# Two groups of 384 columns instead of 448 and 320, and a higher priority for the split of a weight tile

## Chip, cores and metric

The kernel runs on one core of a Trainium2 chip. The metric is the device time of one launch in microseconds (us), the median of several runs. PE is TensorE, PEld its weight loads, DVE is VectorE, ACT is ScalarE, POOL is GpSimd, SP is SyncE, whose queue issues nearly all DMAs here.

## Reference

One inference step of a one-layer decoder with a model width of 1024: 2048 prompt tokens and 8 x 8 sample tokens, 2112 columns in all. What is computed, cut to its skeleton:

```python
proj = rms_norm(x) @ w_in                      # 1024 x 2464, 20 weight tiles
o_attn = sliding_window_attention(rope(q), rope(k), v, sinks)     # window 128
o_rw   = rwkv7(h_rw, ...)                      # recurrent, a 64 x 64 state per head
x = x + rms_norm(concat(o_attn, o_rw) @ w_out) # 8 weight tiles
gu = rms_norm(x) @ w_ffn_in                    # 44 weight tiles
hid = silu(conv3(gu[:, :2816])) * gu[:, 2816:]
x = x + rms_norm(hid @ w_ffn_out)              # 22 weight tiles
```

Everything is float32. The dense products are made of float32r halves: a tensor x is split into hi (rounded) and lo = x - hi, and each product is hi*hi + lo*hi + hi*lo, three matmuls.

## The kernel before

**Dense stages.** The 2112 columns are cut into five groups by `groups` (L61): 448, 448, 448, 448 and 320 columns; the last holds the 64 sample columns. Each group passes four kinds of stage: P (`project`, 20 tasks), O (`outproj`, 8 tasks), and the FFN as two stages, 60 and 6 tasks. A task is one weight tile of 128 x 1024 and 24 matmuls of 128 x 128 weights by the group's columns. All stages run in one written order:

```python
order = [P[0], P[1], P[2], O[0], P[3], F[0], O[1], F[1], P[4], F[2], O[2], F[3],
         O[3], F[4], F[5], O[4], F[6], F[7], F[8], F[9]]
```

F[2g] and F[2g+1] are the two FFN stages of group g.

**The weight tile's way.** `Dense.run` (L392) works on the tasks in order. In task i, after its second step, it emits `halves(i + 2)` (L411) and then `raw(i + 4)` (L406). `raw` is the DMA of a tile into one of two `w` buffers. `halves` takes one of three pairs of buffers `wh`, `wl` and calls `split` (L383): ACT casts w to wh, DVE subtracts to wl. So a split can start when its DMA has landed and when task i - 1, which read the buffers last, is done on PE; the next DMA needs the buffer that the split frees.

**Sides and mixer.** Between dense steps, a `Flow` (L234) emits two other streams of work. Sides are what follows an evicted product: token shift, rotary, `pair` (the factors of the recurrence), norms (`norm` L539, `rms` L805). The mixer does attention and the recurrence in eight units of 256 prompt columns and one for the samples, each in a window that is laid over the dense stages by their calculated cost (`Stage.cost`, L343). A stage can have to wait for others (`cond`, `cond2`): P needs the result of its `norm`, which reads x in `parts_of(n)` pieces (4 x 112 for 448 columns, 4 x 80 for 320, 3 x 128 for 384).

**Order on the engines.** The instructions of sides and mixer on PE stay in program order. On the other queues a scheduler chooses at compile time: each engine takes, of the instructions that are ready in its simulated run, the one with the lowest number of priority, which is the order of emission. `tc.high_priority(200)` sets the number of what is emitted under it 200 lower, so it goes ahead of up to 200 instructions emitted before it, on its engine, if it is ready. On the chip each queue then runs in the order written.

Of the kernel before, what the change touches and what calls it, by code (L numbers as in the profile page):

```python
# [32 lines left out]
CH = 64  # L33
# [3 lines left out]
GW, T, BW = 448, 256, 456  # L37
# [23 lines left out]
def groups(seq):  # L61

    n = seq + NS
    return [(t0, min(GW, n - t0), t0 + GW >= n) for t0 in range(0, n, GW)]


def parts_of(n):
# [13 lines left out]
class Shared:  # L81
# [26 lines left out]
    def derived(self):  # L108
# [17 lines left out]
        nc.gpsimd.memset(self.scanm.rearrange("p (c t) -> p c t", t=CH)[:, :, 0:1], 0.0)  # L126

        t0, n, _ = groups(self.seq)[-1]
        self.scans = cp.tile([128, n], F32, name="scans")
        nc.gpsimd.memset(self.scans, 1.0)  # L130
# [101 lines left out]
class Flow:  # L232
# [81 lines left out]
    def run(self, dense):  # L314
        for c in dense:
            if c is not None:
                self.force(c)
            self.tick()
        self.force(lambda: not (self.sides or self.mix or self.units or self.posts))
# [27 lines left out]
class Dense:  # L347
# [44 lines left out]
    def run(self, stages):  # L392

        nc = self.nc
        tasks = [t for s in stages for t in s.tasks]
        nt = len(tasks)
        raws, parts, starts, i = {}, {}, {}, 0
        for s in stages:
            starts[i] = s
            i += len(s.tasks)  # L400

        def view(i, t):
            m = tasks[i].m
            return t if m is None else t.rearrange("p (k m) -> p k m", m=128)[:, :, :m]

        def raw(i):  # L406
            if i < nt and i not in raws:
                raws[i] = view(i, self.W("w"))
                nc.sync.dma_start(out=raws[i], in_=tasks[i].src)

        def halves(i):  # L411
            if i < nt and i not in parts:
                raw(i)
                parts[i] = [view(i, self.sp.tile([128, D], F32R, tag=x, name=x, bufs=3)) for x in ("wh", "wl")]
                self.split(*parts[i], raws[i])

        first = stages[0]
        for k in range(KT):
            first.fetch(k)
            if k in (2, KT - 1):  # L420
                raw(k // 4)
        first.begin()
        halves(0)
        for k in range(KT):
            first.piece(k)
        yield None
        halves(1)
        for j in range(2, 4):
            raw(j)
        for i, t in enumerate(tasks):  # L430
            n1, n2, n6 = [starts.get(i + j) for j in (1, 2, 6)]
            if n6 and n6.begin:
                n6.begin()
            if n2:
                yield n2.cond
                yield n2.cond2
                if n2.piece:
                    yield from self.hold()
                    for k in range(3):
                        n2.fetch(k)  # L440
            wh, wl = parts[i]
            for k, c in enumerate(t.run(wh, wl)):
                if k == 1:
                    halves(i + 2)
                    raw(i + 4)
                if n1 and n1.piece:
                    n1.piece(k)
                    self.held = k < KT - 1
                yield c
# [44 lines left out]
    def project(self, g):  # L494

        sh, nc, a, v, te = self.sh, self.nc, self.a, self.nc.vector, self.te
        t0, n, sample = groups(sh.seq)[g]
        npr = n - NS if sample else n
        segs = [Seg(0, npr, 1, npr, CH, 0, sh.carry, sh.carry, sh.EC[:, t0 // CH:(t0 + npr) // CH])]
# [340 lines left out]
    def outproj(self, g, need):  # L840

        sh, nc, a, v = self.sh, self.nc, self.a, self.nc.vector
        t0, n, _ = groups(sh.seq)[g]
        m, st = [], {}
        S = Stage(n, cond=lambda: need <= self.done)
# [848 lines left out]
```

## Time and profile before

| | us |
|---|---|
| median of 3 runs | 2902.23 |
| lowest, highest | 2900.92, 2902.95 |
| profiled execution | 2901.7 |
| its span, first to last instruction | 2899.9 |

The profiled execution is 0.5 us under the median, and 1.8 us of it lie outside the span. Its mean granted TensorE clock is 0.965. All rows are of that one execution, and times in them count from the start of the span. A row of waits tells what an engine's idle time ended with.

### The profile page before, as it was taken

Reading aid. Unit: us, or ns where it says so; the run is one execution under the profiler, and the core shown is the slowest. Engines: PE = TensorE matmul, PEld = TensorE weight load, DVE = VectorE, ACT = ScalarE, POOL = GpSimd, SP = SyncE. Lnnn points to the kernel's source line nnn. Section 1 sums busy time; section 2 is a strip of 40 time slices with the busy share of each in tenths; the row PEclk is TensorE's granted clock in tenths of the full one; section 3 lists DMA queues with packets and bytes.
Section 4 is the critical chain, followed back from the end, with each engine's and each line's share of the span. In section 5 each row is a group of like instructions: output and inputs, shape, how many; then the busy total and the mean of one; then the engine's idle time right before and its main releaser. Section 6 shows DMA issues by size and latency. Waiting matters only on the chain.

```text
span 2899.9 us, 46282 instructions
## 1 busy us (share of the span) xinstructions
PE 2749.9 (95%) x16993; PEld 2344.2 (81%) x16993; DVE 1934.6 (67%) x3792; ACT 1410.0 (49%) x2630; POOL 239.9 (8%) x519
## 2 busy tenths in 40 slices
PE   8898995999999999978999999999999999999997
PEld 6676783667888888857887888888899999999997
DVE  6677685586874674696874575788645774557666
ACT  6455553455564455445754446554333453334543
POOL 1011010001000000003100000000001000101111
PEclk9998996799999999989999999999999999999998
DMA  6566664347744434456744335475333563335443
GB/s 211 156 202 168 189 180 128 121 137 219 209 138 140 125 108 148 142 155 188 230 129 136 117 120 169 156 233 164 122 112 107 178 192 109 104 108 182 158 148 120
DMA packets 310530, 446.58 MB, mean 154 GB/s; under 512 B 118536, under 2 KB 238952, under 8 KB 310288
## 3 DMA queue, kind: packets, MB, share of 16 engines
q1 hardware_dynamic: 309872, 443.48, 49.5%
q8 instruction: 134, 2.20, 0.3%
q14 instruction: 92, 0.75, 0.1%
q10 hardware_dynamic: 432, 0.16, 0.0%
HBM read 362.19 MB, written 76.97 MB: 151 GB/s over the span
## 4 chain that ended last, share of the span: by engine, by line
PE 81%; DVE 9%; DMA 4%; issue 3%; ACT 2%; SPq 1%; DVEq 0%; ACTq 0%
PE gm L213 50%; PE pf L213 17%; PE pc L184 3%; PE po L184 1%; DVE wl L386 1%; PE sc L184 1%; PE pz L184 1%; PE ppt L184 1%; SPq L1089 1%; DVE tmp L1075 1%; DVE tt L1076 1%; PE pu L184 1%; PE pS L184 1%; DMA r<-x2d 1%; PE sc_e L184 1%
## 5 line engine op out<-in xcount | busy, mean ns | idle before, releaser
L213 PE MATMUL gm<-xhi,wh 128*128 128x448 f32 (+3 forms) x2880 | 1062.1, 371 | 32.0 <-ACT wh L385 17.2
L213 PE MATMUL gm<-xhi,wl 128*128 128x448 f32 (+3 forms) x2880 | 1035.2, 360 | 11.5 <-DVE wl L386 11.5
L213 PE MATMUL gm<-xlo,wh 128*128 128x448 f32 (+3 forms) x2880 | 1039.5, 361 | 6.5 <-DVE xlo L386 6.1
L385 ACT CAST wh<-w 128x1024 fp32r<-128x1024 f32 (+1 forms) x470 | 489.4, 1042 | 708.0 <-PE gm L213 321.2
L386 DVE TENSOR_TENSOR wl<-w,wh 128x1024 fp32r<-128x1024 f32 (+1 forms) x470 | 569.9, 1213 | 375.3 <-ACT wh L385 362.6
L213 PEld LDWEIGHTS gm<-xhi,wh 128*128 128x128 f32 (+2 forms) x2880 | 543.4, 189 | 117.4 <-issue 30.1
L213 PEld LDWEIGHTS gm<-xlo,wh 128*128 128x128 f32 (+2 forms) x2880 | 544.6, 189 | 60.2 <-DVE xlo L386 12.7
L213 PEld LDWEIGHTS gm<-xhi,wl 128*128 128x128 f32 (+2 forms) x2880 | 544.3, 189 | 57.7 <-DVE wl L386 15.0
L213 PE MATMUL pf<-hh,wh 128*128 128x448 f32 (+1 forms) x880 | 319.5, 363 | 2.1 <-DVE acc L942 1.7
L213 PE MATMUL pf<-hl,wh 128*128 128x448 f32 (+1 forms) x880 | 313.1, 356 | 0.0
L213 PE MATMUL pf<-hh,wl 128*128 128x448 f32 (+1 forms) x880 | 312.6, 355 | 0.0
L915 POOL COPY zcar<-zz 128x2 f32<-128x2 f32 x110 | 79.1, 719 | 1467.4 <-ACT zz L904 1467.4
L942 DVE TENSOR_TENSOR acc<-acc,pf 128x448 f32<-128x448 f32 (+1 forms) x200 | 117.7, 591 | 112.1 <-PE pf L213 111.2
L213 PEld LDWEIGHTS pf<-hh,wh 128*128 128x128 f32 x880 | 165.3, 188 | 25.4 <-issue 6.7
L213 PEld LDWEIGHTS pf<-hh,wl 128*128 128x128 f32 x880 | 165.2, 188 | 12.1 <-issue 0.7
L213 PEld LDWEIGHTS pf<-hl,wh 128*128 128x128 f32 x880 | 165.5, 188 | 11.5 <-issue 1.7
L911 DVE SCALAR_TENSOR_TENSOR c<-zz,c_cw,c 128x448 f32<-128x448 f32 (+1 forms) x220 | 140.8, 640 | 22.4 <-ACT c L905 18.8
L925 DVE TENSOR_TENSOR c<-c,gm 128x448 f32<-128x448 f32 (+1 forms) x110 | 65.1, 592 | 121.0 <-PE gm L213 103.2
L918 ACT ACTIVATE c<-c 128x448 f32<-128x448 f32 (+1 forms) x110 | 61.3, 557 | 126.7 <-DVE c L911 93.4
L1075 DVE TENSOR_TENSOR tmp<-gb,tt 64x31 f32<-64x31 f32 (+21 forms) x279 | 92.2, 331 | 12.4 <-DMA gb<-dgr 8.8
L386 DVE TENSOR_TENSOR xlo<-r,xhi 128x448 fp32r<-128x448 f32 (+1 forms) x112 | 64.2, 591 | 47.8 <-ACT xhi L385 47.6
L1076 DVE TENSOR_TENSOR tt<-tt,tmp 64x31 f32<-64x31 f32 (+21 forms) x279 | 92.4, 331 | 3.5
(272 smaller groups left out, 3082.3 us busy)
## 6 DMA issues: line engine op xcount, KB each, us to landing
w<-in_w SPq DMA_DIRECT2D x220, 512.0 KB
w<-in_w2q SPq DMA_DIRECT2D x100, 512.0 KB
w<-in_w_all SPq DMA_DIRECT2D x90, 512.0 KB
ab<-abd SPq DMA_DIRECT2D x66, 512.0 KB
w<-in_w_out SPq DMA_DIRECT2D x40, 512.0 KB
r<-in_xT SPq DMA_DIRECT2D x56, 224.0 KB
r<-od SPq DMA_DIRECT2D x32, 224.0 KB
x2d<-mx SPq DMA_DIRECT2D x32, 224.0 KB
```

What stands on the lines that cost most here:

```text
L184: return self.tc.keep_in_program_order(f(*args, **kw))
L213: return self.te.matmul(out, lhsT, rhs, **kw)
L385: self.nc.scalar.copy(out=hi, in_=src)
L386: self.nc.vector.tensor_tensor(out=lo, in0=src, in1=hi.bitcast(F32), op=ALU.subtract)
L911: v.scalar_tensor_tensor(out=c[:, :npr], in0=z[:, j:j + npr], scalar=cw(j), in1=c[:, :npr], op0=ALU.mult, op1=ALU.add)
L915: nc.gpsimd.tensor_copy(out=sh.zcar[:, f, :], in_=z[:, npr:npr + 2])
L918: nc.scalar.activation(out=c, in_=c, func=AF.Silu)
L925: v.tensor_tensor(out=c, in0=c, in1=ps, op=ALU.mult)
L942: v.tensor_tensor(out=accs[c], in0=accs[c], in1=ps, op=ALU.add)
L1075: v.tensor_tensor(out=tm, in0=col, in1=row, op=ALU.mult)
L1076: v.tensor_tensor(out=tt[:nb, w:, 0:w], in0=tt[:nb, w:, 0:w], in1=tm, op=ALU.subtract)
L1089: nc.sync.dma_start(out=x, in_=y)
```

## The change

The last two groups get the same width: 768 remaining columns are cut at a multiple of 64, into 384 and 384 (the last keeps the 64 sample columns, and has 320 prompt columns instead of 256). And the two instructions of a weight tile's split are emitted under a higher priority; the tile's DMA is not.

```diff
 def groups(seq):
 
     n = seq + NS
-    return [(t0, min(GW, n - t0), t0 + GW >= n) for t0 in range(0, n, GW)]
+    starts = list(range(0, n, GW))
+    left = n - starts[-2]
+    starts[-1] = starts[-2] + (left + CH) // (2 * CH) * CH
+    return [(t0, t1 - t0, t1 == n) for t0, t1 in zip(starts, starts[1:] + [n])]
...
                 parts[i] = [view(i, self.sp.tile([128, D], F32R, tag=x, name=x, bufs=3)) for x in ("wh", "wl")]
-                self.split(*parts[i], raws[i])
+                with self.tc.high_priority(200):
+                    self.split(*parts[i], raws[i])
```

## Rows read from the trace of the kernel before

**Rows 1.** The page, whole span: busy time of two engines; chain that ended last, by engine.

```profile
PE 2749.9 (95%) x16993; PEld 2344.2 (81%) x16993; DVE 1934.6 (67%) x3792; ACT 1410.0 (49%) x2630; POOL 239.9 (8%) x519
...
PE 81%; DVE 9%; DMA 4%; issue 3%; ACT 2%; SPq 1%; DVEq 0%; ACTq 0%
```

**Rows 2.** Windows by stage: P0; F1; P4; F9. Stretch, length, busy (count), clock, DMA.

```profile
0.00:140.00 140.00, 116.46 (x508) 95.30 (x509) 91.24 (x160) 74.02 (x131) 12.14 (x49) 0.95 0.61 184
...
1203.00:1274.00 71.00, 55.97 (x290) 41.04 (x289) 63.89 (x161) 32.58 (x83) 1.41 (x4) 0.92 0.63 190
1274.00:1399.00 125.00, 110.68 (x884) 94.86 (x885) 91.45 (x216) 69.73 (x161) 31.60 (x63) 0.89 0.58 173
...
2859.00:2900.00 41.00, 23.41 (x156) 22.16 (x154) 25.82 (x59) 9.12 (x15) 0.00 (x0) 0.81 0.30 95
```

**Rows 3.** Windows of steady FFN at 448 and 320 columns: PE, PEld, DVE, ACT, POOL.

```profile
2450.00:2500.00 50.00, 50.00 (x245) 45.56 (x244) 24.89 (x31) 19.42 (x27) 5.35 (x8) 1.00 0.33 106
...
2700.00:2750.00 50.00, 50.00 (x343) 50.00 (x343) 31.54 (x53) 22.75 (x39) 8.14 (x20) 1.00 0.47 151
```

**Rows 4.** Waits of PE, 20 to 140 us (P0): total us, times, longest.

```profile
PE gm L213 <- DVE wl L386: 9.3, 4, 5.6
PE rb_ps L184 <- DVE bk L771: 4.3, 1, 4.3
```

**Rows 5.** Waits of PE, 1274 to 1400 us (P4).

```profile
PE gm L213 <- ACT wh L385: 9.7, 2, 7.7
...
PE gm L213 <- DVE wl L386: 1.3, 2, 1.0
```

**Rows 6.** Timeline of DVE, 86 to 103 us (P0): start, length, instruction.

```profile
95.17 0.62 DVE L513 TENSOR_TENSOR hs<-gm,rb 128x448 f32<-128x448 f32 x1 [4.33 <-PE gm L213]
...
99.50 0.62 DVE L651 TENSOR_TENSOR qk<-qk,qsw 128x448 f32<-128x448 f32 x1
100.04 2.35 DVE L386 TENSOR_TENSOR wl<-w,wh 128x1024 fp32r<-128x1024 f32 x2
```

**Rows 7.** Timeline of PE, 94 to 109 us.

```profile
101.32 0.74 PE L213 MATMUL gm<-xhi,wl 128*128 128x448 f32 x1 [5.56 <-DVE wl L386]
101.86 0.57 PE L213 MATMUL gm<-xhi,wh 128*128 128x448 f32 x1
...
105.59 0.57 PE L213 MATMUL gm<-xlo,wh 128*128 128x448 f32 x1
```

**Rows 8.** Timeline of SP's queue, 1318 to 1342 us (P4).

```profile
1326.23 3.94 SPq L1089 DMA_DIRECT2D G<-dxr  x8
...
1331.68 0.38 SPq L409 DMA_DIRECT2D w<-in_w_all  x1
```

**Rows 9.** Timeline of ACT, the same stretch.

```profile
1337.37 1.04 ACT L385 CAST wh<-w 128x1024 fp32r<-128x1024 f32 x1 [6.02 <-DMA w<-in_w_all]
```

**Rows 10.** Waits of PE, 1203 to 1274 us (F1, ahead of P4).

```profile
PE ms L184 <- DVE sa L803: 5.3, 1, 5.3
PE rb_ps L184 <- DVE dg L568: 5.3, 1, 5.3
```

**Rows 11.** Timeline of DVE, 1264 to 1275 us (the norm ahead of P4).

```profile
1266.79 1.22 DVE L386 TENSOR_TENSOR wl<-w,wh 128x1024 fp32r<-128x1024 f32 x1
...
1269.68 0.48 DVE L568 TENSOR_TENSOR dg<-c_ident,rs 80x320 f32<-80x320 f32 x1
```

**Rows 12.** Waits of ACT, whole span.

```profile
ACT wh L385 <- PE gm L213: 321.2, 166, 8.7
```

**Rows 13.** Groups by line and form, whole span: busy us, mean ns, idle before.

```profile
L386 DVE TENSOR_TENSOR wl<-w,wh 128x1024 fp32r<-128x1024 f32 x460 | 561.7, 1222 | 375.3 <-ACT wh L385 362.6 <-DMA dgr<-G 4.1 <-PE pu L184 4.0
...
L973 DVE SCALAR_TENSOR_TENSOR acc<-acc,c_gT,rb 128x448 f32<-128x448 f32 x32 | 20.9, 676 | 1.4 <-ACT rb L823 1.4
```

**Rows 14.** Groups by line and form, 2875 to 2900 us (the end).

```profile
L973 DVE SCALAR_TENSOR_TENSOR acc<-acc,c_gT,rb 128x320 f32<-128x320 f32 x8 | 4.1, 547 | 2.0 <-ACT rb L823 2.0
```

## The prediction

> **What bounds the kernel now.** I read the page first, for the engine that sets the time: PE is busy for 2749.9 of 2899.9 us and has 81% of the chain that ended last [rows 1]. So the time is PE's work, plus some 150 us in which it stands still, plus what a lowered clock adds to the work after a stop. The reader should see that DVE at 67% over the whole says little, because the next view, the windows by stage, shows where the standing still lies: the FFN stages run PE without a gap [rows 3], while P0 is idle for 140 - 116.5 = 23.5 us, F1 for 15.0, P4 for 14.3 and the last stage for 17.6 [rows 2]. In F1 DVE is busy for 63.9 of 71 us, so there DVE is the bound; in P0 no engine is full, so there it is order and latency. Third, the waits of PE in those windows give the reason of each stop, and fourth, timelines of the queue that was late show what stood ahead of the late instruction. These two views carry the sum.
>
> **The widths: PE.** No instruction count of the dense products changes; each group has 94 tasks of 24 matmuls, 2256, before and after. What could change is the time of one. In two steady FFN windows one matmul goes every 50/245 = 0.204 us at 448 columns and every 50/343 = 0.146 us at 320 [rows 3]. The quotient is 0.714, that of the widths as well (320/448). So the time is proportional to the columns with no fixed part that these rows show, 384 columns should take 0.175 us, and 2 x 0.175 equals 0.204 + 0.146. This term is zero; the counts are whole instructions, so it is known to about 0.5%, and the 0.35 us a pair over 2256 pairs makes that some 4 us either way.
>
> The weight loads do not set a floor in these rows: a load is recorded with 45.56/244 = 0.187 us at 448 columns, and yet matmuls, each with a load of its own, follow each other at 0.146 us at 320 [rows 3]. The Trainium skill, "TensorE: Matmul & The Clock Gate", section "Back-to-back issue gap", says that in a stream of load and matmul pairs the spacing is set by both, which would make a narrow matmul wait for its load. If the recorded 0.187 us were such a floor, two groups of 384 would save 0.204 + 0.187 - 2 x 0.187 = 0.017 us on 2256 pairs, 38 us; the spacing of 0.146 us rules it out nearly entirely.
>
> **The widths: everything else.** DVE and ACT work of the two groups is nearly proportional to columns too, but moves from P3, O3 and the FFN of group 3 to those of group 4. Three effects have a size.
>
> (a) P4 gains slack. A split may run from the end of task i - 1 to the start of task i + 2, two tasks: 48 x 0.146 = 7.0 us now, 8.4 us at 384 columns. It needs 1.04 (the cast [rows 9]) and 1.22 us (the subtraction [rows 13]). This helps the same waits as the priority; I count it there.
>
> (b) The norm ahead of P3 and P4 reads 3 pieces instead of 4. Ahead of P4 PE stands still for 5.3 us until `dg`, the last step of that norm [rows 10]. One piece less is worth at least nothing and at most that whole wait; the yields in `norm` give a piece 3 of about 17 us, so I take 2 us off. Ahead of P3 the norm has a whole O stage as cover: nothing; without that cover it would be the same 2 us.
>
> (c) The end gets longer. After the last matmul come about ten DVE steps on the group's width, then the norm and its output. One step takes 676 ns at 448 and 547 ns at 320 columns [rows 13, 14], 1.0 ns a column, so 384 costs 0.065 us more each: 16 steps of the final norm and some more ahead of it, 1.0 to 1.5 us, plus wider matmuls of the norm at half clock (0.81 granted on average there, 1.2 GHz for a part of it [rows 2]). I take 1.5 us, bounds 1 and 3.
>
> **The priority.** It adds and removes no instruction. It can only take away PE's waits for `wh` and `wl`, and it can only lengthen others, as DVE and ACT do the same work in another order.
>
> In P0 PE waits for `wl` four times, 9.3 us [rows 4]. The longest shows how: `wl` could not start before 100.04 us, because it stood in DVE's queue behind `hs`, which itself waited until 95.17 for PE, and then behind seven further instructions of sides, from `qk` to `qk` [rows 6]. PE stopped for 5.56 us and came back at half clock: ten matmuls in 105.59 - 101.86 = 3.73 us, 0.373 each where 0.204 is the rule, 1.2 instead of 2.4 GHz [rows 7]. That adds (0.373 - 0.204) x 11 = 1.9 us to this stop. P0's weight waits with their clock are about 9.3 + 3 = 12 us. In P4 it is 9.7 + 1.3 = 11.0 us [rows 5]; at a mean clock of 0.89 over 125 us [rows 2] 13.8 us of full clock are missing, nearly half of that while PE stands still anyhow, so about 5 us go with the weight waits. P4 together: 16 us. The most that the priority and the slack can take away is 28 us; the least is nothing, if the scheduler put the splits late because in its run their data was late.
>
> What of it is queue order? In P0 the subtraction was passed over by work emitted earlier, which 200 numbers of priority reach; but the cast ahead of it was late too, and a transfer that is late in the scheduler's run is not helped. I take half, 6 us. In P4 7.7 of the 11.0 us are one stop, and that one is a DMA's: ACT waited 6.0 us for w [rows 9], whose DMA was issued at 1331.68 behind eight issues of the recurrence that held SP for 3.9 us and others ahead [rows 8]. The DMA's priority is not raised; an earlier split frees its buffer earlier and may let it be issued ahead of that block. With its clock this stop is some 11 us; I take a third, 4 us. The rest of P4, 3.3 us and 1.5 of clock, is queue order at ACT and DVE: 5 us, all of it.
>
> Against that, what does a split that goes first delay? Behind it stand the sides and the mixer's evictions. In the FFN stages PE has no waits that it could lengthen, the lags of the mixer cover 1.2 us. But ahead of P1, P2 and P4, PE waits for a chain on DVE: 4.3 us ahead of P1 [rows 4], and ahead of P4 5.3 us for `sa` and 5.3 us for `dg` [rows 10]. Already now one `wl` of 1.22 us lies in the chain that ends with that `dg` [rows 11]. I count one more split for each of these three places, 3.7 us with the clock about 4. Bounds: nothing, and 15 us (three splits at each place are 11 us, and 4 us of half clock).
>
> **Sum.** -6 - 4 - 5 (weight waits) - 2 (norm) + 1.5 (end) + 4 (delays) = -11.5 us. Against the profiled execution's own 2901.7 us this gives 2890.2; the median stands 0.5 us above that execution, so 2891 us, -0.4%.
>
> **Rivals.**
>
> *The waits move.* The splits come earlier and PE stops at the next thing that is late: in P0 the norm ahead of P1, in P4 the recurrence's transfers. For it speaks that no engine's work shrinks and that P4's largest stop is a DMA's [rows 9]; against it that P0's `wl` had its operands long before [rows 6]. Time: 2902 within 6 us.
>
> *Slower: split first, chain late.* Place: F1 and the start of P4, where DVE has no room (63.9 of 71 us). Each split put ahead delays a chain that PE already waits for by 1.22 us. ACT stands idle for 321 us in front of casts whose buffer PE has not yet freed, 166 times [rows 12]; a cast that is put still earlier in ACT's queue holds up what follows it. The skill's same page, section "Architectural detail", states that ACT's and DVE's queues are strictly first in, first out; the trace agrees, since `wl` stood behind a waiting `hs` [rows 6]. It decides as soon as the chains of the three places lose more than the 15.5 us that the other terms give: four more splits at each, 14.6 us, with the clock. If PE merely waits for the chain where it waited for weights, three at each are enough: 2902 + 11 + 4 - 2 + 1.5, about 2916 us.
>
> *Much faster.* All weight waits go, the block at SP included, and P4's norm is no longer waited for: -28 - 5 + 1.5, 2870 us.
>
> *The narrow matmuls had a floor:* 2902 - 38, 2864 us; the spacing speaks against it.
>
> **How the numbers follow.** About 0.2% (6 us) is what a measurement of this kernel can tell from no change. My forecast, faster by 6 to 20 us: 0.42. Much faster: 0.12, and the floor 0.02. The waits move, within 6 us: 0.21. Slower: 0.23, because after P3 the emission of all sides and units shifts as well. So faster 0.56, same 0.21, slower 0.23. The likeliest case alone reaches from 2882 to 2896. The range takes in the rival below nearly whole and the one above up to its worked-out time: 2869 to 2916.
>
> **What would show it.** In the changed profile: matmuls of group 3 and 4 every 0.175 us, with the dense time of both together unchanged; PE's waits for `wh` and `wl` in P0 and P4 below 12 us instead of 20; the stop at 101 us gone or short; the wait for `dg` ahead of P4 within 3 us of today's 5.3; the stretch after the last matmul 1 to 2 us longer. Wrong would be the forecast if the waits for `dg`, `bk` and `sa` grew by more than those for weights shrank, if SP still held P4's weights back for 8 us, or if the mixer's units fell elsewhere after P3 and opened a stop that today's trace does not have.

## The result, and the profile after

The changed kernel takes 2924.96 us, median of 4 runs (2920.32 to 2932.91), where the kernel before takes 2902.59 beside it (2900.92 to 2904.54, 4 runs): a ratio of 1.0072, interval 1.0054 to 1.0090. That is slower by 21 us, above the whole range that was forecast. Below, a ratio is always against the kernel before on the same chip, and 0.1% is 2.9 us. One profiled execution stands within some 8 us of its kernel's median, so totals are read from ratios and places from profiles. That of the changed kernel took 2932.9 us; its span is 2931.1.

The page of the kernel after, its busy time and its chain, beside [rows 1]:

```profile
PE 2767.6 (94%) x16979; PEld 2392.5 (82%) x16979; DVE 1939.8 (66%) x3792; ACT 1412.0 (48%) x2618; POOL 241.4 (8%) x519
...
PE 43%; DVE 3%; DMA 2%; issue 1%; ACT 0%; SPq 0%; DVEq 0%; ACTq 0%
```

PE's busy time grew by 17.7 us for the same products, and the span without busy time from 150.0 to 163.5 us. So the loss of this execution has two halves: more standing still, and matmuls that take longer, at a lower granted clock (0.957 over the execution, 0.965 before). A part of the second half belongs to this execution alone, which is 8 us above its median: in O0 it has 40.7 us at the lower clock where the kernel before had 28.2, with 5.3 and 5.0 us of standing still. The chain could be followed back only through half of the span this time and is not used.

Windows of the kernel after, in order P0, P1, F1, P4, steady FFN at 384 columns, and the last stage (columns as in [rows 2]):

```profile
0.00:123.00 123.00, 112.08 (x507) 92.52 (x508) 91.11 (x159) 74.34 (x131) 14.58 (x49) 1.00 0.70 205
123.00:287.00 164.00, 141.05 (x779) 109.33 (x779) 120.77 (x254) 82.68 (x182) 18.76 (x38) 0.91 0.62 177
1204.00:1276.00 72.00, 59.28 (x286) 44.36 (x285) 59.32 (x137) 29.66 (x70) 1.82 (x4) 0.85 0.64 192
1276.00:1426.00 150.00, 135.06 (x984) 111.98 (x984) 111.96 (x261) 81.75 (x184) 19.42 (x68) 0.91 0.55 167
2632.00:2884.00 252.00, 251.87 (x1450) 251.31 (x1449) 149.06 (x249) 108.40 (x181) 40.45 (x86) 1.00 0.44 139
2884.00:2931.00 47.00, 27.87 (x154) 26.35 (x152) 28.98 (x58) 9.46 (x15) 0.00 (x0) 0.82 0.28 90
```

P0 ends at 123 instead of 140 us, with full clock. P1 takes 164 us where it took 156. P4 holds 984 matmuls in 150 us; before it held 884 in 125 [rows 2]. The steady FFN gives 252/1450 = 0.174 us a matmul, as forecast.

PE's waits after, first in P0 (20 to 123 us), then in P1, then in P4 (1276 to 1426 us):

```profile
PE gm L216 <- DVE wl L389: 0.5, 1, 0.5
```

```profile
PE pz L187 <- DMA zt<-dtr: 9.9, 5, 7.2
PE pd L187 <- ACT tha L755: 5.6, 1, 5.6
PE rb_ps L187 <- DVE bk L775: 3.8, 1, 3.8
```

```profile
PE ppt L187 <- DVE nr L53: 7.7, 1, 7.7
PE ss_ps L187 <- ACT k L618: 4.3, 1, 4.3
PE gm L216 <- ACT xhi L388: 2.8, 1, 2.8
```

The waits for weights are gone: 9.3 us in P0 have become 0.5 [rows 4], 11.0 in P4 none [rows 5]. The priority did what it says. In P4 two new ones of 7.7 and 4.3 us stand in their place (`xhi` had 3.2 us before), and in P1 there is a new one of 5.6 us for `tha`. PE stands still in P4 for 14.9 us, before for 13.9.

### The profile page after: what moved, and what is told of

The parts are those of the page before. It is cut to its first block, busy times and chain, and to the rows that moved or that the text cites. A ratio compares the mean times of both kernels' runs of the same rounds, so it can differ in the third digit from the quotient of the medians.

```text
span 2931.1 us, 46214 instructions
## 1 busy us (share of the span) xinstructions
PE 2767.6 (94%) x16979; PEld 2392.5 (82%) x16979; DVE 1939.8 (66%) x3792; ACT 1412.0 (48%) x2618; POOL 241.4 (8%) x519
## 5 line engine op out<-in xcount | busy, mean ns | idle before, releaser
L216 PE MATMUL gm<-xlo,wh 128*128 128x448 f32 (+4 forms) x2880 | 1040.1, 362 | 2.8 <-DVE xlo L389 2.7
L216 PE MATMUL gm<-xhi,wl 128*128 128x448 f32 (+4 forms) x2880 | 1037.0, 360 | 0.8 <-DVE wl L389 0.8
L919 POOL COPY zcar<-zz 128x2 f32<-128x2 f32 x110 | 87.0, 791 | 1464.0 <-ACT zz L908 1464.0
L915 DVE SCALAR_TENSOR_TENSOR c<-zz,c_cw,c 128x448 f32<-128x448 f32 (+2 forms) x220 | 140.8, 640 | 15.9 <-ACT c L909 13.3
```

Of the source, the lines that this page charges most:

```text
L216: return self.te.matmul(out, lhsT, rhs, **kw)
L915: v.scalar_tensor_tensor(out=c[:, :npr], in0=z[:, j:j + npr], scalar=cw(j), in1=c[:, :npr], op0=ALU.mult, op1=ALU.add)
L919: nc.gpsimd.tensor_copy(out=sh.zcar[:, f, :], in_=z[:, npr:npr + 2])
```

## Experiments

"Old widths" are those of the kernel before.

**The two parts alone.** The first kernel has only the diff in `groups`, the second only the priority.

> The widths alone: groups of 384 and 384, no priority. If the loss of 22 us comes from the widths (the mixer's and the sides' work falls elsewhere after P3), this takes 2915 to 2930 us, with the waits for wh and wl in P0 as before (9.3 us) and new stops only after 606 us. If the loss comes from the priority, it takes 2895 to 2906 us. If the two only lose together, both parts alone are near 2903.

> The priority alone: groups of 448 and 320. If the loss comes from the priority, this takes 2912 to 2930 us, with P0 about 17 us shorter and P1, P2 and O0 together as much longer, so that O0 ends at 606 to 609 us, and with further loss in P4 or after. If the loss comes from the widths, it takes 2885 to 2905 us: P0's gain is given back by the end of O0, P4's weight waits go.

Widths alone: ratio 1.0051 (1.0033 to 1.0069). Priority alone: 1.0037 (1.0023 to 1.0052). Both lose, and their sum, 0.88%, is within the interval of the whole change. So as far as these intervals tell, the two losses add up, and each can be studied alone.

**Is any other order of work a loss?** The spacing between steps of the sides is a little longer:

```diff
-    LAG, GAP = 2500.0, 1400.0
+    LAG, GAP = 2500.0, 1500.0
```

> Old widths, no priority; the shortest spacing that the emission keeps between steps of the sides is 1500 instead of 1400 of its units. No work changes, on PE steps of sides move by some matmuls, the counts by stage stay, DVE has about a quarter of its instructions elsewhere. Theory C (the kernel before is one of few good arrangements, and any other costs some us in new small stops): 2907 to 2916 us, with stops in other places. Rival D (a change of order alone is worth little, and widths and priority lost for reasons of their own): 2899 to 2906 us.

Ratio 0.9989 (0.9973 to 1.0004). Rival D holds for this one other order: it costs nothing. That any other order would cost something is not borne out, and the reasons are looked for in the two parts themselves.

**The priority, by place.** First the 20 tiles of P0 alone, then those of P0 and P4, then all but P1's:

```diff
-                with self.tc.high_priority(200):
+                with self.tc.high_priority(200 if i < len(first.tasks) else 0):
```

> Old widths; the split has its higher priority only for the 20 weight tiles of P0, all later tiles keep the old order. With the priority everywhere P0 ended 17 us earlier, and at the end of O0 9 us of it were left. Theory A (later splits pass later chains): without them P1, P2 and O0 lose little, so O0 ends 9 to 17 us before that of the kernel before and the rest is as before: 2885 to 2893 us. Rival B (what is won in P0 is waited away in P1 to O0, because the chain of the first units sets their end): O0 ends less than 5 us earlier, 2898 to 2904 us.

> Old widths, the split's priority for the tiles of P0 and of P4, the two stages whose weight waits the prediction counted. If P4's 11 us of weight waits are worth anything by themselves: 5 to 10 us below the kernel with P0's tiles alone, 2883 to 2889 us against a kernel before of 2902. If other chains stand right behind them, as P4 with all tiles raised took the same 125 us: within 4 us of that kernel, 2889 to 2897 us.

> Old widths, the split's priority everywhere but for P1's 20 tiles (transfers as they are). The kernel with P0's tiles alone gained 10 us, the one with all tiles lost 7. If nearly all of these 17 us is P1's, as the profiles have it (10 us by stage, the rest within what clock and chance move): 2892 to 2900 us, P1 at 153 to 157 us. If later stages lose as much by their own splits: 2901 to 2908 us.

The ratios are 0.9965 (0.9952 to 0.9978), 0.9961 (0.9946 to 0.9975) and 1.0000 (0.9985 to 1.0016). So P0's part gains 10 us; it is P1 and the other stages that lose. Durations of the stages in the profiles, us, each from its first dense matmul to the next stage's (P0 from the start):

```
                     P0     P1     P2    P3     F0    P4   |  ratio
before             139.9  156.1  215.4  160.1  387.8 125.0 |  1
P0 alone           123.4  153.3  223.1  165.4  388.9 125.5 |  0.9965
P0 and P4          123.1  154.1  225.3  165.6  389.8 123.7 |  0.9961
all but P1         121.9  153.8  221.3  164.7  392.0 124.3 |  1.0000
all                123.0  163.3  219.8  164.6  390.9 125.1 |  1.0037
```

P0 gains 17 us, and 8 of them are given back in P2 (it takes 219 us or more in every profile whose P0 takes 125 us or less, and 213 to 216 in the others whose second group is as before). P3's 5 us are not the priority's: the kernel with the longer spacing has them too (165.6 us). With all tiles raised P1 loses 10 us. "All but P1" does not have that loss, and yet the kernel as a whole has not P0's gain either, which the first guess (nearly all in P1) did not expect: some 10 us go to the splits from P2 on, in small amounts. By the profiles, PE stands still for 150.6 us in all where it is 142.5 with P0 alone, most of it in P3 (14.8 instead of 10.4 us) and F0 (3.4 instead of 1.5).

Two kinds of wait grew most: for `h`, an eviction on ACT, and for `dg`, the last step of a norm on DVE. PE's waits over the whole span, with P0 alone and with all but P1:

```profile
PE gm L213 <- ACT h L709: 2.9, 3, 1.4
PE ms L184 <- DVE dg L818: 3.0, 1, 3.0
```

```profile
PE gm L213 <- ACT h L709: 11.7, 5, 5.9
PE ms L184 <- DVE dg L818: 10.0, 4, 3.2
```

Against these 15.8 us, waits for `wh` went from 18.0 to 10.4 us and others shrank too.

P4's waits, with P0's tiles raised, and with P0's and P4's:

```profile
PE gm L213 <- ACT wh L385: 10.3, 2, 8.4
```

```profile
PE gm L213 <- ACT h L709: 5.0, 2, 4.0
PE gm L213 <- ACT xhi L385: 3.0, 2, 2.7
...
PE gm L213 <- ACT wh L385: 1.7, 1, 1.7
```

Of 11.6 us of waits for weights (10.3 for `wh`, 1.3 for `wl`) 9.9 go, PE stands still in P4 for 10.5 instead of 14.0 us, P4 takes 1.8 us less, and the kernel is not measurably faster. Of the longest new stop, for `h` until 1294.28 us, ACT's timeline (P0 and P4 raised) shows what stands ahead: two casts, which ended at 1291.38, and a softmax behind them.

```profile
1289.39 1.99 ACT L385 CAST wh<-w 128x1024 fp32r<-128x1024 f32 x2 [1.29 <-PE gm L213]
...
1293.77 0.46 ACT L709 COPY h<-gm 64x256 f32<-64x256 f32 x2
```

Right behind P4's weight waits stood other waits, which took up about two thirds of what was won.

**The priority, by engine.** The cast and the subtraction raised one at a time (the call of `split` written out, one of its two lines under the priority).

> Old widths; only the subtraction on DVE has the higher priority, the cast on ACT keeps the old order. P0's waits were for wl, which is DVE's. Theory A1 (the loss comes from casts that stand first in ACT's queue and wait for a buffer): P0 keeps most of its 17 us and the stops for ACT's evictions do not come, 2888 to 2897 us. Rival A2 (the loss comes from DVE's chains that a split passes): as with the whole priority, 2907 to 2916 us.

> Old widths; only the cast on ACT has the higher priority, the subtraction on DVE keeps the old order. Theory A1 (ACT's queue carries the loss): stops of PE for ACT's h, tha and xhi come as with the whole priority, and P0's waits for wl stay, so 2905 to 2916 us. Rival A2 (DVE's queue carries it): 2898 to 2905 us.

DVE alone: 1.0013 (1.0000 to 1.0025); ACT alone: 0.9996 (0.9982 to 1.0009). With DVE alone P0 takes 122.8 us and P1 165.1, as with both; with ACT alone 132.8 and 154.4. So the subtraction alone brings P0's whole gain and P1's whole loss, as A2 has it (the cast alone brings 7 of P0's 17 us and no loss in P1). In the total it costs less than both raised together, 0.13% against 0.37%, so the cast has a share in what is lost elsewhere. The two waits named above go by engine: with DVE alone raised PE waits 8.6 us for that `dg` and 3.2 for `h`, with ACT alone 3.0 and 7.3, with both 10.3 and 11.7. What the raising does to DVE's queue is in the group of `wl`: busy, mean, then idle time ahead of it and for what. Before, DVE alone, ACT alone:

```profile
L386 DVE TENSOR_TENSOR wl<-w,wh 128x1024 fp32r<-128x1024 f32 (+1 forms) x470 | 569.9, 1213 | 375.3 <-ACT wh L385 362.6 <-DMA dgr<-G 4.1 <-PE pu L184 4.0
```

```profile
L417 DVE TENSOR_TENSOR wl<-w,wh 128x1024 fp32r<-128x1024 f32 (+1 forms) x470 | 569.9, 1213 | 409.6 <-ACT wh L415 407.9 <-issue 0.3
```

```profile
L417 DVE TENSOR_TENSOR wl<-w,wh 128x1024 fp32r<-128x1024 f32 (+1 forms) x470 | 569.8, 1213 | 382.5 <-ACT wh L416 379.0 <-DMA abd<-bk 0.9 <-DMA r<-in_xT 0.8
```

A raised subtraction stands first in DVE's queue before its cast is done: 45 us more of waiting for `wh`, in which DVE does nothing. (Whether the work behind it in the queue was ready by then, these rows do not show.)

**Which order costs P1 its 10 us?** Timelines of the kernel after, whose P1 goes like that of the priority alone (164.1 and 163.3 us): SP's queue, then ACT, then DVE.

```profile
223.85 0.88 SPq L562 DMA_DIRECT2D r<-in_x  x2
...
228.56 0.74 SPq L1422 DMA_DIRECT2D out_o_v_s<-in_cv  x1
246.55 0.51 SPq L1086 DMA_DIRECT2D dxr<-gb  x1
...
247.75 0.62 SPq L412 DMA_DIRECT2D w<-in_w_l  x1
...
263.89 2.61 SPq L562 DMA_DIRECT2D r<-in_x  x2
...
270.41 0.80 SPq L562 DMA_DIRECT2D r<-in_x  x2
```

```profile
252.21 0.62 ACT L388 CAST wh<-w 128x512 fp32r<-128x512 f32 x1 [5.68 <-DMA w<-in_w_l]
```

```profile
252.86 0.69 DVE L389 TENSOR_TENSOR wl<-w,wh 128x512 fp32r<-128x512 f32 x1 [8.42 <-ACT wh L388]
...
273.81 0.46 DVE L569 TENSOR_TENSOR ss<-ss 112x4 f32<-112x4 f32 x2 [2.73 <-ACT r L565]
```

SP issues nothing from 229.3 to 246.55 us: it stands at `dxr`, a transfer of the recurrence that waits for `gb`. Behind it stand P2's first weight tile, for which ACT and DVE then wait with nothing else ahead of it, and five pieces of x for the norm ahead of P2 (`r`, issued only from 263.89 on). That norm's sum starts at 273.81 us, 13 us before P1's end; with the priority for P0 alone it starts at 245.89 us:

```profile
245.89 0.14 DVE L566 TENSOR_TENSOR ss<-ss 112x4 f32<-112x4 f32 x1
```

The stop of SP at `dxr` goes with the raised subtractions of P1: it is 16.7 us with DVE alone raised, 4.7 with ACT alone, and 2.2 with all tiles but P1's.

The first guess was the weight tile. The kernel with the whole priority at old widths, and its transfer raised too:

```diff
+                with self.tc.high_priority(200 if i == 40 else 0):
-                nc.sync.dma_start(out=raws[i], in_=tasks[i].src)
+                    nc.sync.dma_start(out=raws[i], in_=tasks[i].src)
```

> Old widths, the split's priority everywhere, and besides one transfer, that of P2's first weight tile w_l, raised by the same 200. With the priority alone this transfer stands on SP behind the recurrence's dxr, which waits for gb until 246.6 us; ACT's cast and DVE's subtraction of that tile, put first in their queues, wait for it until 252.3 and 252.9 us, and PE stops for 7.2 us for zt. Theory E (the loss of P1 is this one order of two transfers: a split put first in line for data that is late): P1 takes 154 to 157 us as with P0's tiles alone instead of 163, DVE has no idle stretch of 8 us there, the whole 2901 to 2907 us. Rival F (the loss is spread over many splits that pass chains): P1 stays at 160 us or more, 2908 to 2914 us.

Ratio 1.0063 (1.0049 to 1.0076), and P1 takes 162.2 us. SP and DVE in it:

```profile
229.99 0.62 SPq L410 DMA_DIRECT2D w<-in_w_l  x1
246.90 0.51 SPq L1084 DMA_DIRECT2D dxr<-gb  x1
...
263.95 0.90 SPq L560 DMA_DIRECT2D r<-in_x  x2
```

```profile
247.42 0.69 DVE L386 TENSOR_TENSOR wl<-w,wh 128x512 fp32r<-128x512 f32 x1 [2.64 <-ACT wh L385]
```

The tile comes early, DVE's stop falls from 8.4 to 2.6 us, and P1 is no better: theory E falls. (Why the total is worse by another 0.26% than with the priority alone stays open.) What stayed late are the pieces of x. So these next, in `norm`:

```diff
+                        with self.tc.high_priority(200 if g == 2 else 0):
-                        nc.sync.dma_start(out=xts[-1][:w], in_=a["x"][t0 + w * i:t0 + w * i + w, x:y])
+                            nc.sync.dma_start(out=xts[-1][:w], in_=a["x"][t0 + w * i:t0 + w * i + w, x:y])
```

> Old widths, the split's priority everywhere, and besides the transfers of x for the norm ahead of P2 raised by the same 200, so that on SP they stand ahead of dxr again, as in the kernel before. With the split's priority alone five of them are issued only from 264 to 270.5 us, after SP has stood at dxr for 17 us, and that norm comes 20 us later than with the priority in P0 alone. Theory E2 (P1's loss is this one order on SP): P1 takes 153 to 157 us instead of 163, and the whole 2901 to 2907 us. Rival F (the splits themselves, ahead in DVE's queue, delay P1's chains): P1 stays at 160 us or more, the whole 2908 to 2916 us.

Ratio 1.0014 (1.0003 to 1.0025), 2908.81 beside 2905.89 us (the kernel before took 4 us more on this chip than the 2902 that the expectation reckoned with; without that correction the total would lie in rival F's range), so 0.23% below the priority alone. P1's window, and SP in it:

```profile
125.00:279.00 154.00, 139.79 (x779) 108.45 (x777) 119.91 (x255) 83.72 (x184) 23.27 (x38) 0.91 0.67 190
```

```profile
231.04 2.11 SPq L560 DMA_DIRECT2D r<-in_x  x2
233.68 0.62 SPq L409 DMA_DIRECT2D w<-in_w_l  x1
250.50 0.46 SPq L1084 DMA_DIRECT2D dxr<-gb  x1
```

Here are SP's waits at `dxr` in P1, of the kernel after and of this one:

```profile
SPq L1086 <- ACT gb L1083: 17.2, 1, 17.2
```

```profile
SPq L1084 <- ACT gb L1081: 1.8, 1, 1.8
```

And the norm's sum on DVE in this kernel:

```profile
247.13 0.15 DVE L567 TENSOR_TENSOR ss<-ss 112x4 f32<-112x4 f32 x1
```

With the pieces of x ahead of `dxr`, the norm starts as early as with P0 alone and P1 has its 154 us back, with every split raised as before. This much of the loss is shown: one order on SP's queue. What is left, 0.14% above the kernel before and 0.49% above P0 alone, lies elsewhere.

**All weight transfers raised.**

```diff
+                with self.tc.high_priority(200):
-                nc.sync.dma_start(out=raws[i], in_=tasks[i].src)
+                    nc.sync.dma_start(out=raws[i], in_=tasks[i].src)
```

> Old widths, the split's priority everywhere, and every weight tile's transfer raised by the same 200, so that it goes ahead of the transfers of sides and mixer. Theory E (splits lose where they stand first and their data is late): all such stops go, 2890 to 2900 us, at or below the kernel with the priority in P0 alone. Rival F (splits lose by passing chains on DVE, and transfers ahead of the recurrence's delay its chains as well): 2908 to 2918 us.

Ratio 1.0109 (1.0092 to 1.0125), 2932.5 us, the slowest with old widths and above both forecasts. P1 has its 156.2 us, but P0 loses the gain (139.9 us, 25.1 idle) and P3, F0, O2 and O4 are 4 to 6 us longer each than before. Raising a transfer is no cure in itself. (That it loses by passing other transfers in SP's queue was argued, not shown.)

**The widths.** New widths with the priority for P0 alone; new widths with a later start of one unit of the mixer (`(f(F[2], 0.3), f(F[2], 0.47))` in place of `(f(F[2], 0), f(F[2], 0.47))`); and the 64 columns taken from the second group in place of the fourth (`starts[2:] = [t - CH for t in starts[2:]]`).

> New widths, the split's priority only for P0's 20 tiles. If the two parts add up, the widths' +0.5% and this priority's -0.35% give 2904 to 2910 us against 2902 to 2907 of the kernel before. If widths lose only where the schedule of before was lucky and another order of the start moves that too, 2892 to 2902 us.

> New widths, old priority; the sixth unit of the mixer may start only at 0.3 instead of 0 of F2 (in the emission's count of dense work, which runs ahead of the stage itself), so that F1 and P4 hold fewer of the mixer's matmuls: about halfway back to the count of before. Theory G (the widths lose by what the longer P4 takes in): half of the loss goes, 2905 to 2911 us, and P4 shortens by some 7 us while F2 lengthens by less. Rival H (what moves into P4 is missing in F2, and the loss lies in stops spread over O2, O3, F6 and the end): 2912 to 2919 us.

> Old priority; widths 448, 384, 448, 448 and 384: the last group as in the change, but the 64 columns are taken from the second group and not from the fourth. Stages P1, O1, F2 and F3 become narrower in place of P3, O3, F6 and F7. Theory H (a narrower fourth group covers too little of what lies beside O2, O3 and the start of F6): those three stages go back to the kernel before, 9 to 14 us less than with the change's widths, so 2898 to 2908 us but for what P1 and P2 lose or win, which here depend on the narrower second group. Rival I (the wider last group is what costs, in P4 and at the end): 2912 us or more, with the same stops in O2, O3 and F6.

The ratios are 1.0020 (1.0008 to 1.0033), 1.0043 (1.0030 to 1.0057) and 1.0104 (1.0082 to 1.0125). The first stands 0.55% above the same priority at old widths: the widths cost some 15 us whatever the order at the start. Time of a stage beyond its dense matmuls (some 0.2036 us for one of 448 columns, and for others in proportion), us:

```
                   F1    P4    F2    O2    F3    O3    O4    F6    F8    F9
before            42.2  55.2  88.8  12.6  14.4  11.1   4.1   4.1   4.3  19.9
P0 alone          44.2  55.7  90.0  12.6  14.4  10.8   3.9   5.1   5.0  20.1
widths            39.9  70.6  83.5  16.9  16.2  15.3   1.3  10.4   0.9  21.7
widths, P0        38.7  67.5  82.4  17.0  16.2  13.9   1.4   9.2   0.7  21.7
widths, later     34.9  60.8  92.4  20.0  16.5  11.7   1.3  13.6   0.9  21.5
second group      37.8  66.3  80.2  22.0  19.1  18.0   1.4  10.3   1.0  21.6
after             42.9  66.8  84.0  13.3  16.0  11.8   1.4  14.9   0.7  21.9
```

What P4 takes in more (11 to 15 us but for the later start) is mostly missing elsewhere, in F1, F2, O4, F8 and P3 (62.4 before, 58.2 with the widths alone). Moved out of P4 by the later start, it comes back in F2 and O2: theory G is not supported, though the median is 2 us lower, within the intervals. What does not come back lies in O2, O3, F6 and F9: with the widths alone 4.3, 4.2, 6.3 and 1.8 us (in the kernel after nearly all in F6 and F9). With the second group narrower and the fourth as before they are not smaller, O2 and O3 larger. That speaks for rival I in O2 and O3: they go with the wider last group rather than with the narrower fourth one. In F6 it is otherwise. There PE stands still for 5.3 us with the widths alone and for 2.2 in this kernel, one wait of 2.0 us for `xhi`, which the kernel before has too (2.2 us, at the end of O4). So the stops that the widths add in F6 need the narrower fourth group; what is longer there in this kernel is in part time at a lower clock (0.92 in the first 42 us). (It also loses 30 us in O0 and gains 21 in P2, so its total tells nothing.)

At the start of F6 one collision can be seen. Windows of the first 42 us, before and with the widths alone:

```profile
2318.00:2360.00 42.00, 41.37 (x207) 36.70 (x208) 34.03 (x76) 22.29 (x38) 2.60 (x6) 1.00 0.65 202
```

```profile
2328.00:2370.00 42.00, 38.85 (x221) 37.08 (x220) 35.24 (x72) 22.96 (x41) 2.64 (x6) 1.00 0.65 210
```

One of some four such steps per tile in the last group's norm on DVE at that place, before and with the widths alone:

```profile
L869 DVE SCALAR_TENSOR_TENSOR mx<-mx,c_gT,rb 128x320 f32<-128x320 f32 x8 | 4.1, 546 | 0.0
```

```profile
L872 DVE SCALAR_TENSOR_TENSOR mx<-mx,c_gT,rb 128x384 f32<-128x384 f32 x8 | 4.7, 611 | 0.0
```

PE's waits in 2328 to 2400 us with the widths alone:

```profile
PE pf L216 <- DVE c L928: 1.9, 1, 1.9
PE gm L216 <- ACT c L908: 1.6, 1, 1.6
PE gm L216 <- ACT xhi L388: 1.5, 1, 1.5
```

And in the first 100 us of F6 with the second group narrowed, where a norm of 384 columns stands beside an FFN of 448:

```profile
PE gm L215 <- ACT xhi L387: 2.0, 1, 2.0
PE gm L215 <- DVE xlo L388: 0.2, 1, 0.2
```

While group 3's FFN begins, DVE is busy for 84% (before 81%) with group 4's norm, now wider, beside it, and PE waits for `c`, a step of the FFN. The wider norm alone does not bring these waits: beside the FFN of 448 columns there is none for `c`. A narrower FFN asks for its tiles more often (in the 42 us DVE makes 10 splits with the widths, 7 before), and the two together may be the cause. That was argued from these rows; no run takes the norm's steps away. What makes O2 and O3 longer was not settled.

## Why the prediction was wrong

*Widths, PE: right.* 0.174 us measured at 384 columns, 0.175 forecast; the term is zero, and the rival of a floor is out.

*Widths, the rest: the step that failed first.* "DVE and ACT work of the two groups is nearly proportional to columns too, but moves" was taken as free. The term was put at nothing with no reason but that the sum of the work stays; what the work stands beside was not asked. The widths cost 0.51 to 0.55%, 15 to 16 us, seen as longer O2, O3, F6 and F9; by which mechanism stays open but for the end. Of the three effects given a size, the end is right (1.9 us in F9, forecast 1.5), P4's slack can't be told from the rest, and the norm's -2 us is not shown: with the widths alone F1 takes 69.2 instead of 71.5 us and the wait for `dg` is gone, but one of 6.4 us for `acc` stands in its place; in the kernel after F1 takes 72.2 us.

*Priority, P0: right, too small.* The stage gains 17 us and the kernel 10, forecast 6. Not only weight waits go: the 4.3 us for `bk` at P0's end [rows 4] go too, and with them all 13 us at 1.2 GHz (granted clock 1.00 instead of 0.95). That the stage's other stops were the same lateness fits, but no run shows it by itself.

*Priority, P4: wrong.* 9 us were forecast; the waits went nearly whole and the time hardly moved (0.9961 against 0.9965). For this stage the rival "the waits move" was right, though with other waits than the recurrence's transfers that it named.

*Priority, delays: the decisive step.* "I count one more split for each of these three places", 4 us, bounds 0 and 15. Measured, the priority on all later tiles costs 0.72% against P0 alone, 21 us, beyond the bound. And a good part of it was not where, nor how, that step had it. 7 us (by the raised transfers of x) to 11 us (by leaving P1 out) are one order on SP, which no split passes through: with the subtraction raised, `dxr` comes ahead of the norm's transfers, and SP stands 17 us. The prediction read SP only in P4, for what an earlier split would let through [rows 8], and not for what it would push back. The Trainium skill, "Perfetto Trace Analysis", section "DMA Instruction — HWDGE (DVE, Sync)", puts the wait for semaphores ahead of a DMA issue's recorded start and frees the sequencer for the next instruction only at its recorded end; the trace agrees, with nothing issued in the 17.2 us. The other 10 to 14 us, spread over the later stages, have the mark of the rival "split first, chain late": the waits for `dg` grow where the subtraction is raised and those for `h` where the cast is. They were not placed one by one, and no run takes them away.

*The sum.* Measured: P0 -10, P4 0, P1's order and the later splits together +21 (7 and 14, or 11 and 10), widths with the end +15: +26 by the parts, +21 by the whole, whose interval reaches to 26. The rival that forecast 2916 us had the right sign and its first mechanism, a queue's head that waits, but at F1 and P4, and on DVE and ACT alone.

## What to carry to other kernels

A higher priority at compile time can move every queue that the scheduler fills, also those that the raised instructions are not in: here SP's. Before using it, list each in-order queue, DMA issue first, and ask which instruction with a long wait may come forward in it; then raise only where a wait was seen to be queue order, and look stage by stage: here the 20 tiles of P0 gain 0.35%, and all tiles lose 0.37%. Columns that move from one group to another were free on PE, and yet cost 0.5%: ask what the moved work stands beside where it arrives.

## What was not expected of the hardware

One DMA issue that waits held SP's whole queue for 17.2 us, and the norm whose transfers stood behind it began 28 us later than with the priority for P0 alone (273.81 against 245.89 us). And the clock is not the same in two executions of one order: O0, up to which the kernel before and the one with the longer spacing have the same instructions in the same order, took 95.1 us with 28.2 us at the lower granted clock in one profile (0.85 over the stage) and 90.7 with 17.1 in the other (0.91), at 5.0 and 5.4 us of standing still.
